# High parts of the experts' weight tiles: a rounding copy on ScalarE in place of GpSimd

## The chip, the cores and the metric

The kernel runs on one core of a Trainium2 chip. The metric is the device time of one execution in microseconds, the median of several runs; less is better. The engines are named as in the profile: PE (TensorE), DVE (VectorE), ACT (ScalarE), POOL (GpSimd), SP (SyncE, which issues the loads of the weights).

## The reference

One sequence of 512 tokens of 1024 features goes through two layers of a first block (stick breaking and sliding window attention, an MLP) and one layer of a second (a state space mixer and a sparse attention side by side, then a mixture of experts) and a last norm. All is float32. What the change concerns is the mixture of experts:

```python
p_group = softmax(tf @ w_rg + b_rg);  pg, gsel = top_k(p_group, 1)
pe = softmax(logits of the chosen group);  pv, pi = top_k(pe, EXPERT_TOPK)
wts = pg * pv / sum(pv)
combine = sum(one_hot(ids, N_EXPERTS) * wts[..., None], axis=1)
for e in range(N_EXPERTS):                       # 32 experts
    he = silu(t @ w_g[e]) * (t @ w_u[e])         # 1024 -> 256
    out = out + combine[:, e:e + 1] * (he @ w_d[e])
```

Each token goes to two experts of one group of eight. The kernel computes an expert only for the tokens that chose it.

## The kernel before

**Products in parts.** To keep nearly float32's precision, most products are made of fp32r operands: a value x is cut into hi (x rounded to fp32r) and lo = x - hi, and x w is taken as x hi + x lo, and so on. `split` (with `hi_pool` at line 187 on POOL or `hi_act` at line 190 on ACT for hi, and `lo_dve` at line 193 on DVE for lo) does this everywhere. With `act=False`, the default, hi is a tensor_scalar of POOL (x times 1 times 1); with `act=True` it is a copy of ACT.

**Weights.** All weights come through `Weights`, as 532 tiles of 128x1024 in one fixed order. `load` issues a tile's DMA on SP's queue; `prefetch` cuts a tile that has been loaded; `tile` hands out the next one and sees to it that the one after it is cut too. In the experts' part a tile's raw slot and its slots for parts come from `slots` and `parts`: the raw slots are a ring of 17 (tiles named S and w_st in the trace) and a few outside it, the parts go by turns into two rings, w_hi/w_lo (two slots) and m_hi/m_lo (three). `hold` keeps the experts' tiles uncut, though loaded, until the routing is under way.

**Experts.** An expert has six tiles: four with gate and up columns, two with rows of the down product. The first five are cut, the last is used whole (as fp32). So the 32 experts have 192 tiles of 512 KB and 160 cuts. `gather` builds, for a quad of experts, the matrix S (gS) that selects the tokens in their slots, on DVE (lines 1916 and 1917), multiplies it with the normalised rows on PE (ps_tr), and ACT copies the results out of two banks into xT (line 1926). `expert` multiplies xT by the gate and up tiles (ps_gu); ACT copies the result (mcp, line 1940), PE transposes it by a product with an identity (ps_pt), ACT takes Silu (mhe), DVE multiplies by the up half (lines 1947 and 1949); the hidden values are cut into mhs (hi on POOL, lo on DVE), and PE multiplies them by the down tiles (ps_po). `pair` scales two experts' rows by the tokens' weights (line 2010), and `put` scatters them to DRAM by an indirect DMA on POOL's queue.

**Before the first quad** stands the routing: `route`, a chain of small DVE steps with a few products; the normalised rows (`moe`: ACT scales, POOL adds the shift at line 2064, ACT makes hi, DVE lo); `turn`, which turns h into rows by PE and ACT. The first five tiles are cut inside `tc.issue_after(...)`, which puts what is issued within it behind the named instruction: in the kernel before, behind `chosen` (the last step of the first gS, on DVE) and `shifted` (the last addition of the shift, on POOL).

**Order.** The program gives the instructions an order of priority; a scheduler with a timeline of its own then fixes the order of each engine's queue, and each queue runs in that order, waiting by semaphores. The branch for experts with more than 64 tokens (`further`) is not entered with these inputs.

Of the kernel before, what the change touches and what calls it, by code (L numbers as in the profile page):

```python
# [11 lines left out]
F32R = mybir.dt.float32r  # L12
# [3 lines left out]
OP = mybir.AluOpType  # L16
# [12 lines left out]
# ---------------------------------------------------------------- constants  # L29
# [4 lines left out]
# 1 / theta ** (i / 64) and theta ** (-i / 64), i = 0, 2, .. 62, as float32 gives them  # L34
# [32 lines left out]
class Weights:  # L67
    """Tiles of 1024 columns per partition, taken in one fixed order."""
# [3 lines left out]
    def __init__(self, k, src, total):  # L72
        self.k, self.src, self.total = k, src, total
        self.specs = []
        self.raw, self.ready = {}, {}
        self.loaded = self.made = 0
        self.hold = total       # no tile from here on is cut yet
        self.slots = None       # a part of the program may place tile i itself: slots(i) -> raw, parts (None: not cut)
# [10 lines left out]
    def prefetch(self, upto):  # L89
        k = self.k  # L90
        self.load(upto)
        for i in range(self.made, min(upto, self.hold)):
# [10 lines left out]
            k.split(hi, lo, st)  # L103
# [29 lines left out]
class K:  # L133
# [7 lines left out]
    def phase(self, name, alias={}, nbufs={}):  # L141
        """Opens the working pools of a part of the program."""
        self.alias, self.nbufs = alias, nbufs
        ctx = ExitStack()
        self.wk = ctx.enter_context(self.tc.tile_pool(name="wk_" + name, bufs=1, reuse_waits="tile"))
        self.ps = ctx.enter_context(self.tc.tile_pool(name="ps_" + name, bufs=1, space=PSUM, reuse_waits="tile"))
        return ctx

# [5 lines left out]
    def t(self, shape, tag, dt=F32, bufs=1):  # L154
        """Kept: the slots S0.. and the constants; the rest goes when its phase ends."""
# [11 lines left out]
    def pace(self, every, back=2):  # L167
        """Beats for the products of dense units: each waits for the one `back` before it (0: none).
        They keep the queue of TensorE short, for the steps of a chain between them."""
# [19 lines left out]
    def hi_act(self, hi, x):  # L189
        self.nc.scalar.copy(hi, x)  # L190
# [18 lines left out]
    def rsqrt(self, out, v):  # L209
        """out = v ** -0.5, v [128, n]."""  # L210
        self.nc.gpsimd.tensor_tensor(out, v, self.mhalf.to_broadcast(list(v.shape)), op=OP.pow)

    def rsqrt_act(self, out, v, w, y):
        """The same by ScalarE and VectorE; w and y are scratch of the same shape (y may be out)."""
# [22 lines left out]
    def fm(self, rhs, pieces, evac):  # L237
        """A unit: 128 output features by 512 tokens."""
# [6 lines left out]
    def dense_tm(self, xh, xl, outs, pieces_of, ncols, bank_mates=1):  # L245
        """outs[tb] [128 tokens, ncols] += x[:, tb].T @ w; `bank_mates` outputs share a bank."""
# [38 lines left out]
    def norm_chunk(self, c, x, g, hi, lo):  # L285
        """x [128, 512] of chunk c: g x in two parts, and its squares into the running sum."""
# [16 lines left out]
    def norm_factor(self):  # L303
        """r[token], token major."""
# [12 lines left out]
    def norm_finish(self):  # L317
        """r[token] token major and along the free axis on all partitions."""
# [12 lines left out]
    def o_halves(self, dst, ps_lo, ps_hi, shape):  # L331
        """dst = ps_lo + ps_hi for the two 64-partition halves of a bank."""
# [5 lines left out]
# ---------------------------------------------------------------- first block  # L338
class Block1:
    # dense units between the steps of the stick breaking attention  # L340
    PRE = 6
    PLAN = {3: ("q", 4), 4: ("q", 5), 6: ("g", 6), 7: ("q", 6), 8: ("q", 7), 10: ("g", 7)}
    PACE = (3, 2)       # of the dense units, but for the first
# [88 lines left out]
    def swa_turn(self, tb):  # L432
        """Transposes of q and k of one token block."""
# [75 lines left out]
    def swa(self, r):  # L509
        """Token blocks in a pipeline of four stages, dense units between them."""  # L510
# [154 lines left out]
    def attend(self, xh, xl):  # L665
        """xh, xl [128, 8*512]: parts of g x; the running sum of squares is in k.ssq."""
# [23 lines left out]
    def merge(self, xs, gt, rb):  # L690
# [16 lines left out]
        for m in range(8):  # L707
            g1 = g1s[m // 2][:, m % 2]

            def both(m=m, g1=g1):  # L710
                a, b = k.bank("w2", 2, (P, 2, 512)), None
                # the two branches fill one tile of eight blocks
# [21 lines left out]
    def out_and_mlp(self, ms, x_src, next_norm, between=()):  # L734
        """x_src: DRAM [128, 8, 512]; next_norm(c, x_c) takes each finished chunk of the new x;
        `between` is work for the gaps between the units."""
# [54 lines left out]
G, HG = 4, 8          # state space groups, heads in each  # L791
# [3 lines left out]
def shape_constants2():  # L795
    i = np.arange(P)
    causal = np.where(i[:, None] > i[None, :], np.float32(NEG), np.float32(0))   # [s, t]
# [19 lines left out]
def vec_layout(inp):  # L817
    """Small vectors, features on partitions."""
# [12 lines left out]
class Block2:  # L831
# [7 lines left out]
    def row(self, name, at, n, tag):  # L839
        """A vector of the input on all partitions."""  # L840
# [33 lines left out]
    def scale(self, c, x):  # L874
        """x of chunk c by the first norm's gain."""
# [3 lines left out]
    def norm(self, x, rb, hi, lo):  # L879
        """Parts of the first modulated norm, chunk by chunk, of x by the gain."""  # L880
        k, nc = self.k, self.k.nc
        for c in range(KC):
# [3 lines left out]
            if c == KC - 1:  # L886
                # its gain comes here, and not in place: it is still on its way to DRAM
# [8 lines left out]
    def begin(self, hh, hl):  # L896
        """Steps of the state space and gates of the attention, for all tokens."""
# [20 lines left out]
    def ssm_steps(self):  # L918
        """The step sizes, and the decays' running sums within a chunk, tokens on partitions."""
# [26 lines left out]
    def ssm_begin(self):  # L946
        k, nc = self.k, self.k.nc
        # the running sums along the free axis
# [10 lines left out]
        # dt x by parts, beside zeros, so that two heads fill the partitions of a product  # L959
# [11 lines left out]
    def ssm_units(self, g, room):  # L971
        """Units of a group's projections: B, C, four of x, four of z; room(i) takes the i-th."""
# [16 lines left out]
    # units taken ahead of the attention's end, whose results wait in DRAM  # L989
    AHEAD = {0: range(10), 3: range(8, 10)}  # L990
    PACE = (4, 2)       # of the dense units between the attention's steps
# [34 lines left out]
    def ssm_scan(self, g, xz, bc):  # L1026
# [3 lines left out]
        BC = s6[:, 0:2048].rearrange("p (a b t) -> p a b t", a=2, b=2)      # B, C by parts  # L1030
# [5 lines left out]
        def front(ck):  # L1036
            """What no state enters: dt x by parts, D x, and the decayed products of C and B."""
# [30 lines left out]
        for ck in range(4):  # L1068
# [33 lines left out]
            for b in range(2):  # L1102
                # two pairs of heads: features on partitions, the products with both parts of M side by side
# [25 lines left out]
    def ssm_norm(self, g, xz, ssq):  # L1129
        """Norm over the group's features, by parts."""  # L1130
# [45 lines left out]
    def ssm(self):  # L1176
        """The state space, and the gated sum of both mixers by parts."""
# [26 lines left out]
    def gate_units(self, col, tag):  # L1204
        """Columns of the input projection before their sigmoid: the tile, and the units that fill it."""
# [14 lines left out]
    def rotations(self, work):  # L1220
        """cos | cos and -sin | sin of every token and frequency."""
# [29 lines left out]
    def rotate(self, dst, src, tb, n, tmp):  # L1251
        """dst [128, n, 64] = src turned by position."""
# [8 lines left out]
    def by_token(self, hh, hl, cols, n, tag="d"):  # L1261
        """x @ columns of the input weights, tokens on partitions, n <= 256 columns."""
# [7 lines left out]
    def nsa_keys(self, sw, kr, tb):  # L1270
        """Keys of both groups, by parts, each twice over the partitions."""
# [12 lines left out]
    def nsa_values(self, br, src, tb):  # L1284
        """Values of the selected branch by parts, those of the window whole."""
# [37 lines left out]
    def blocks(self, kcT, vcT):  # L1323
        """Blocks of keys and values with their position vectors, by parts: [128, key or value, 16, 2, 64]."""
# [19 lines left out]
    def compress(self, blocks, more):  # L1344
        k, nc = self.k, self.k.nc
        # both parts of the blocks on the partitions, then their sum turned
# [23 lines left out]
        hv = k.t([P, 2, 2, 2, P], "hidv", F32R)         # each value block's columns four times  # L1370
# [23 lines left out]
        # values of the compressed blocks, once for each of four heads, beside zeros  # L1394
# [889 lines left out]
```

## Time and profile before

| | |
|---|---|
| median of 3 runs | 2909.4 us (2905.84 to 2910.61) |
| profiled execution: span from first to last instruction | 2902.1 us |
| mean granted TensorE clock over the span | 0.978 |
| PE busy | 2737.3 us (94%) |
| DVE busy | 1893.7 us (65%) |
| POOL busy | 1330.9 us (46%) |
| ACT busy | 840.2 us (29%) |
| moved over the span | 355.47 MB, 122 GB/s |

The page gives busy time over the whole span, in which stages with different limits follow one another: the first block, the two mixers, and from about 2440 us the routing and the experts. A view by stretches shows a stage by itself. The view of waits says who stood, for how long, and what ended it. A timeline row is a start, a duration, the engine, the line, the operation with output and inputs, the shape, and how many like it follow one another; in brackets stands the engine's idle time ahead of it and what ended that. The granted clock is a share of 2.4 GHz: 1.00 is the upper level and a half the lower, and values between are means over a stretch with both.

### The profile page before, as it was taken

The page shows a single profiled execution, that of the slowest core. Times are in us where ns is not written, and L with a number is a line of the kernel's source. Part 1 is how long each engine was busy: PE and PEld are TensorE (multiplying, and loading weights), DVE is VectorE, ACT ScalarE, POOL GpSimd, SP SyncE. Part 2 cuts the span into 40 slices and gives each one's busy share as a digit, 9 for nine tenths or more (in the row PEclk, how much of TensorE's full clock was granted, in tenths as well). Part 3 has the DMA queues.
Part 4 walks back from the last instruction along what each step waited for, and adds up shares of the span by engine and source line. Part 5 has one row for each costly group of instructions (what it writes and reads, how often), then busy time and mean ns, then how long its engine had stood idle before and what let it go on. Part 6 is the DMA issues. An engine that isn't in the chain of part 4 may idle for free. (4 is left out here: it accounts for less than half of the span.)

```text
span 2902.1 us, 36642 instructions
## 1 busy us (share of the span) xinstructions
PE 2737.3 (94%) x13452; PEld 2211.3 (76%) x13452; DVE 1893.7 (65%) x2911; ACT 840.2 (29%) x1684; POOL 1330.9 (46%) x1718
## 2 busy tenths in 40 slices
PE   7999999999999999999989999999999997888886
PEld 6788788888878877778869887768787876666664
DVE  6865553334486656556545785668677765999898
ACT  3444221021144441201112354462442333211111
POOL 4544244142355423423323454446655652565665
PEclk9999999999999999999999999999999998999988
DMA  4111332223211124556442411222121252677765
GB/s 136 56 61 51 116 95 95 95 99 112 101 59 59 50 96 147 172 176 196 154 154 95 134 56 48 91 85 77 66 80 66 76 211 77 223 270 262 257 236 207
DMA packets 108875, 355.47 MB, mean 122 GB/s; under 512 B 19495, under 2 KB 20391, under 8 KB 108048
## 3 DMA queue, kind: packets, MB, share of 16 engines
q1 hardware_dynamic: 105056, 342.71, 35.3%
q0 software_dynamic: 2592, 6.15, 0.6%
q10 hardware_dynamic: 1040, 4.19, 0.4%
q8 instruction: 108, 1.77, 0.3%
q14 instruction: 79, 0.65, 0.1%
HBM read 329.51 MB, written 27.26 MB: 123 GB/s over the span
## 5 line engine op out<-in xcount | busy, mean ns | idle before, releaser
L165 PE MATMUL ps_d<-S,w_hi 128*128 128x512 f32 x4448 | 1421.0, 397 | 18.6 <-POOL c_eps L181 5.7
L165 PEld LDWEIGHTS ps_d<-S,w_hi 128*128 128x128 f32 x4448 | 827.7, 188 | 204.4 <-POOL c_eps L181 12.2
L165 PE MATMUL ps_d<-S,w_lo 128*128 128x512 f32 x2224 | 877.0, 396 | 14.9 <-DVE w_lo L193 14.6
L187 POOL TENSOR_SCALAR w_hi<-w_st 128x1024 fp32r<-128x1024 f32 x343 | 389.3, 1135 | 743.3 <-PE ps_d L165 610.6
L193 DVE TENSOR_TENSOR w_lo<-w_st,w_hi 128x1024 fp32r<-128x1024 f32 x343 | 453.8, 1323 | 295.4 <-POOL w_hi L187 273.3
L165 PEld LDWEIGHTS ps_d<-S,w_lo 128*128 128x128 f32 x2224 | 418.8, 188 | 112.9 <-DVE w_lo L193 23.2
L203 ACT ACTIVATE f<-ps_d 128x512 f32<-128x512 f32 x64 | 38.4, 600 | 457.3 <-PE ps_d L165 457.3
L181 POOL MEMSET c_eps<- 1x1 f32 x424 | 35.7, 89 | 233.9 <-PE ps_d L165 197.0
L187 POOL TENSOR_SCALAR m_hi<-S 128x1024 fp32r<-128x1024 f32 x81 | 118.4, 1466 | 52.8 <-PE ps_po L165 22.7
L187 POOL TENSOR_SCALAR S<-of 128x512 fp32r<-128x512 f32 x96 | 105.7, 1101 | 67.5 <-DVE of L728 31.3
L193 DVE TENSOR_TENSOR m_lo<-S,m_hi 128x1024 fp32r<-128x1024 f32 x81 | 124.4, 1549 | 13.8 <-POOL m_hi L187 13.8
L862 DVE SCALAR_TENSOR_TENSOR W<-wada,W 128x1024 f32<-128x1024 f32 x48 | 68.5, 1426 | 97.8 <-DMA wada<-in_w_ada_t 97.8
L1501 POOL TENSOR_SCALAR pw<-pw,ri,gn 128x128 f32<-128x128 f32 (+3 forms) x128 | 90.5, 714 | 54.9 <-DVE ri L1500 49.9
L165 PE MATMUL ps_tr<-gS,S 128*128 128x256 f32 x512 | 87.3, 311 | 24.0 <-DVE gS L1917 24.0
L165 PEld LDWEIGHTS ps_tr<-gS,S 128*128 128x128 f32 x512 | 77.9, 208 | 35.8 <-issue 30.4
L193 DVE TENSOR_TENSOR S<-of,S 128x512 fp32r<-128x512 f32 x96 | 79.5, 828 | 33.0 <-POOL S L187 31.0
L165 PE MATMUL ps_w<-w_hi,S 128*128 128x512 f32 x256 | 83.6, 406 | 10.5 <-POOL w_hi L187 10.5
L193 DVE TENSOR_TENSOR w_lo<-S,w_hi 128x1024 fp32r<-128x1024 f32 x53 | 85.9, 1626 | 2.2 <-POOL w_hi L187 2.2
L187 POOL TENSOR_SCALAR w_hi<-S 128x1024 fp32r<-128x1024 f32 x53 | 68.6, 1296 | 26.8 <-PE ps_gu L165 26.8
L165 PE MATMUL ps_w<-S,w_hi 128*128 128x512 f32 x256 | 80.7, 395 | 0.0
L203 ACT ACTIVATE pw<-pw,mx 128x128 f32<-128x128 f32 (+3 forms) x128 | 71.4, 559 | 29.7 <-DVE mx L1498 28.9
L165 PE MATMUL ps_po<-m_hi,mhs 128*128 128x512 f32 x128 | 50.4, 435 | 29.9 <-DVE mhs L193 24.3
(565 smaller groups left out, 4850.2 us busy)
## 6 DMA issues: line engine op xcount, KB each, us to landing
w_st<-in_w SPq DMA_DIRECT2D x374, 512.0 KB, 3.3
S<-in_w SPq DMA_DIRECT2D x158, 512.0 KB, 4.9
wada<-in_w_ada_t SPq DMA_DIRECT2D x48, 512.0 KB, 3.6
x<-S SPq DMA_DIRECT2D x16, 256.0 KB, 2.0
moe_rows<-S ACTq DMA_DIRECT2D x1, 4096.0 KB, 16.5
ssm_away<-nf SPq DMA_DIRECT2D x12, 256.0 KB, 2.0
S<-in_x_t SPq DMA_DIRECT2D x8, 256.0 KB, 6.9
S<-in_x_t SPq DMA_DIRECT2D x1, 2048.0 KB, 8.0
```

The source lines that it names most:

```text
L165: return self.nc.tensor.matmul(out, l, r, start=start, stop=stop, skip_group_check=sk)
L181: b = self.nc.gpsimd.memset(self.beat_at[:, i:i + 1], 0.0)
L187: self.nc.gpsimd.tensor_scalar(hi, x, 1.0, 1.0, op0=OP.mult, op1=OP.mult)
L193: return self.nc.vector.tensor_tensor(lo, x, hi.bitcast(F32), op=OP.subtract)
L203: i = self.nc.scalar.activation(out, x, f, bias=bias, scale=scale, **kw)
L862: nc.vector.scalar_tensor_tensor(junk, w, 1.0, self.cs, op0=OP.mult, op1=OP.mult, accum_out=self.ada[:, j:j + 1])
L1501: nc.gpsimd.tensor_scalar(w, w, ri[:, c], gate[:, c], op0=OP.mult, op1=OP.mult)
```

## The change

hi of the experts' weight tiles is made by ACT: `Weights` gets a flag `act`, false until `moe` sets it, which `prefetch` hands to `split`. The first five cuts are put behind `turned`, the last hi that ACT made by then (that of the last block of the normalised rows), where it was `shifted`; `chosen` stays. The hi of mhs and all cuts ahead of the experts stay where they are. The rest of the diff takes comments out.

```diff
 class Weights:
     def __init__(self, k, src, total):
...
-        self.hold = total       # no tile from here on is cut yet
-        self.slots = None       # a part of the program may place tile i itself: slots(i) -> raw, parts (None: not cut)
+        self.hold = total
+        self.slots = None
+        self.act = False
...
     def prefetch(self, upto):
...
-            k.split(hi, lo, st)
+            k.split(hi, lo, st, act=self.act)
             self.ready[i] = (hi, lo)
...
     def hi_act(self, hi, x):
-        self.nc.scalar.copy(hi, x)
+        self.last_hi = self.nc.scalar.copy(hi, x)
...
     def moe(self, h, hm, out):
...
-            shifted = nc.gpsimd.tensor_tensor(f, f, shift, op=OP.add)
+            nc.gpsimd.tensor_tensor(f, f, shift, op=OP.add)
             k.split(self.hn_tm[0][:, tb], self.hn_tm[1][:, tb], f, act=True)
...
         self.turn(h, put)
+        turned = k.last_hi
...
         tile0 = len(k.W.specs)
+        k.W.act = True
...
                 k.W.hold = k.W.total
-                with k.tc.issue_after(self.chosen.ins), k.tc.issue_after(shifted.ins):
+                with k.tc.issue_after(self.chosen.ins), k.tc.issue_after(turned.ins):
                     k.W.prefetch(tile0 + 5)
```

## Rows read from the trace of the kernel before

**Rows 1.** Busy time by stretch: start:end, length, busy us (instructions), clock, DMA share, GB/s.
```profile
core 0: us, PE busy (x) PEld busy (x) DVE busy (x) ACT busy (x) POOL busy (x), PEclk, DMA share, GB/s
2472.00:2872.00 400.00, 343.15 (x1617) 263.82 (x1618) 360.36 (x357) 72.96 (x196) 249.10 (x202) 0.93 0.74 250
...
2670.00:2680.00 10.00, 7.96 (x33) 7.21 (x34) 8.11 (x11) 1.02 (x3) 2.13 (x3) 0.66 0.60 205
```
**Rows 2.** Waits of PE, 2472 to 2872: who, for whom, total us, times, longest.
```profile
PE ps_tr L165 <- DVE gS L1917: 24.0, 6, 6.3
PE ps_po L165 <- DVE mhs L193: 22.0, 9, 3.3
PE ps_gu L165 <- DVE m_lo L193: 6.5, 12, 0.7
PE ps_po L165 <- POOL mhs L187: 5.6, 4, 2.1
```
**Rows 3.** Groups on DVE, 2472 to 2872: shapes, count, busy us, mean ns, idle before.
```profile
L193 DVE TENSOR_TENSOR m_lo<-S,m_hi 128x1024 fp32r<-128x1024 f32 x81 | 124.4, 1549 | 13.8 <-POOL m_hi L187 13.8
L193 DVE TENSOR_TENSOR w_lo<-S,w_hi 128x1024 fp32r<-128x1024 f32 x53 | 85.9, 1626 | 2.2 <-POOL w_hi L187 2.2
L193 DVE TENSOR_TENSOR mhs<-mhe,mhs 128x64 fp32r<-128x64 f32 x31 | 44.7, 1442 | 14.1 <-POOL mhs L187 13.8
L1917 DVE SCALAR_TENSOR_TENSOR gS<-moe_c,gq,gS 128x256 fp32r<-128x256 f32 x31 | 27.0, 914 | 0.0
...
L1949 DVE TENSOR_TENSOR mhd<-mhe,ps_pt 128x64 f32<-128x64 f32 x31 | 6.5, 209 | 0.0
```
**Rows 4.** Timeline, 2640 to 2692: rows of DVE, then of POOL.
```profile
2645.64 3.06 DVE L193 TENSOR_TENSOR mhs<-mhe,mhs 128x64 fp32r<-128x64 f32 x1 [1.23 <-POOL mhs L187]
...
2655.58 2.05 DVE L193 TENSOR_TENSOR w_lo<-S,w_hi 128x1024 fp32r<-128x1024 f32 x1
...
2647.59 1.03 POOL L187 TENSOR_SCALAR m_hi<-S 128x1024 fp32r<-128x1024 f32 x1
...
2655.50 1.05 POOL L187 TENSOR_SCALAR m_hi<-S 128x1024 fp32r<-128x1024 f32 x1
2656.51 2.02 POOL L187 TENSOR_SCALAR w_hi<-S 128x1024 fp32r<-128x1024 f32 x1
```
**Rows 5.** Timeline ahead of the first gather: rows of ACT, then of DVE.
```profile
2464.29 2.03 ACT L190 CAST S<-S 128x1024 fp32r<-128x1024 f32 x2
...
2463.79 1.22 DVE L193 TENSOR_TENSOR S<-S,S 128x1024 fp32r<-128x1024 f32 x1
...
2471.45 1.67 DVE L1917 SCALAR_TENSOR_TENSOR gS<-moe_c,gq,gS 128x256 fp32r<-128x256 f32 x4
```
**Rows 6.** Groups on ACT, 2472 to 2872, as in Rows 3.
```profile
L1926 ACT CAST S<-ps_tr 128x256 fp32r<-128x256 f32 x128 | 43.2, 377 | 117.4 <-PE ps_tr L165 100.2 <-PE ps_gu L165 16.6
L1940 ACT COPY mcp<-ps_gu 128x512 f32<-128x512 f32 x32 | 18.8, 588 | 105.1 <-PE ps_gu L165 105.1
...
L203 ACT ACT_TABLE_LOAD x1 | 1.3, 1283 | 0.0
```
**Rows 7.** Timeline of the routing: a row of POOL, then of DVE.
```profile
2459.24 2.21 POOL L187 TENSOR_SCALAR m_hi<-S 128x1024 fp32r<-128x1024 f32 x2
...
2458.29 1.25 DVE L1845 TENSOR_TENSOR st<-A,moe_c 128x256 f32<-128x256 f32 x1
...
2462.82 0.40 DVE L1845 TENSOR_TENSOR st<-A,C 128x256 f32<-128x256 f32 x1
```
**Rows 8.** Waits of SP's queue, 2520 to 2850; then a stretch as in Rows 1.
```profile
SPq L85 <- DVE w_lo L193: 115.9, 48, 9.1
...
2380.00:2390.00 10.00, 8.29 (x29) 6.23 (x28) 4.26 (x4) 0.85 (x2) 2.71 (x2) 0.83 1.00 390
```
**Rows 9.** Groups on POOL, 2472 to 2872, as in Rows 3.
```profile
L187 POOL TENSOR_SCALAR m_hi<-S 128x1024 fp32r<-128x1024 f32 x78 | 115.1, 1479 | 52.8 <-PE ps_po L165 22.7 <-DMA S<-in_w 19.3 <-PE ps_gu L165 6.4
L187 POOL TENSOR_SCALAR w_hi<-S 128x1024 fp32r<-128x1024 f32 x51 | 66.4, 1306 | 26.8 <-PE ps_gu L165 26.8
```

## What the change will do to the time

> **What bounds the kernel now.** The change touches one stage: the 32 experts, where 192 weight tiles of 128x1024 are loaded and 160 of them are cut into a high part (hi: rounded to fp32r) and a low part (lo: what is left). So I read the profile from that stage, not from the page's averages, on which PE is the fullest engine.
>
> First the busy time by stretch, from the first gather of tokens (2472 us) to the last expert's products (2872 us) [rows 1]. In these 400 us PE is busy 343.15, DVE 360.36, POOL 249.10, ACT 72.96, and the 16 DMA engines 74%. DVE is the fullest and PE has 56.9 us of idle time; the granted clock is 0.93 in the mean, and 0.66 in the 10 us that follow a long stop of PE. So PE loses in two ways: it stands, and afterwards it runs slowly. Its work at full clock is about 343 x 0.93 = 319 us: an estimate of the floor that PE sets for this stretch.
>
> Then who ended PE's idle time [rows 2]: the selection matrix gS of the next gather (24.0 us), the low part of an expert's hidden values mhs (22.0), lo parts of weights (6.5) and the high part of mhs (5.6). These four are 58 us, all that PE stands (the first of the waits begins a little ahead of 2472). Every one is an output of DVE or POOL; none of ACT.
>
> Then why DVE is late [rows 3]. A lo part of 128x1024 takes 1549 ns in the mean in one ring and 1626 in the other. The lo of mhs, of 64 columns only, takes 1442 ns, while the product beside it with as many columns takes 209. The time is no arithmetic. The timelines show what it is [rows 4]: a lo takes 2.05 us at 2655.58 where POOL makes hi parts at the same time (1.05, then 2.02), and the lo of mhs takes 3.06 from 2645.64 and ends as the last of a run of POOL's hi parts ends (2647.59 + 1.03). DVE and POOL stop each other. Ahead of the stage [rows 5], while POOL does nothing, a lo takes 1.22 us although ACT runs a cast of the same size at the same time (two in 2.03), and gS's second step takes 1.67/4 = 0.42 against 0.914 in [rows 3].
>
> The Trainium skill ("SBUF — State Buffer", "Who interferes with whom") says that a VectorE instruction with two SBUF inputs contends with a GpSimd instruction that reads SBUF, that the loser blocks until the other has finished, and that ACT waits for nobody. The mutual stop agrees with [rows 4], but the loser's price does not: by the rule the lo of mhs would wait for one hi at most (an estimate of some 1.0 + 0.2 us) and the row shows a wait for a run of them, 3.06. By the rule alone the gain on mhs would be at most 31 x 1.0; the sum below goes by the rows.
>
> **What the change does, part by part.**
>
> (a) 160 hi parts leave POOL. On DVE, 160 lo at 1.22 instead of some 1.57 gives back 160 x 0.35 = 56 us; 31 lo of mhs at about 0.21 (their neighbour of the same size, [rows 3]) instead of 1.44, 38 us; 31 steps of gS at 0.42 instead of 0.91, 15 us. DVE falls from 360 to some 250 us. What stays on POOL (the 64-column hi of mhs, the scattering of rows) still stops DVE now and then; I leave 5 us for it. DVE is then far below PE's 319 and bounds nothing.
>
> (b) PE gets its idle time back, bounded above by all of it: 400 - 319 = 81 us (56.9 of idle, 24 of clock). Below, the bound is nothing, if something else comes late in DVE's place.
>
> (c) ACT gets 160 casts. At 2.03/2 = 1.02 us each [rows 5] that is 163 us: 73 + 163 = 236 us of load, under PE's floor, so ACT bounds by its sum nothing either. But its queue runs in order, and ACT also brings PE what it needs [rows 6]: 128 copies out of the gather's banks (377 ns) and 32 of mcp, which the transposing products wait for (588). Silu (one per expert) stands between them, and its table is loaded once in the whole stage (x1): casts and copies between Silus force no further load. A copy that comes ready behind a running cast waits up to 1.02 us, on average half of that, and it meets a cast in 163/340 of the cases: 0.24 us. With 32 mcp, 32 Silus and 64 pairs of gather copies this is 128 x 0.24 = 31 us if PE has nothing else meanwhile, and 0 if the next expert's products or the next gather fill each gap. No row shows a cast among these copies; I take half, 16 us, since gathers and products do stand mixed on PE, and keep 0 to 31 for the range.
>
> (d) The chain of a weight tile (hi, lo, product) gets no longer: 1.02 on ACT instead of 1.05 to 2.0 on POOL, then 1.22 on DVE instead of up to 2.05. The five slots for parts stay.
>
> (e) The start. The first five hi parts stand on POOL at 2456 to 2461.4, in the middle of the routing, and stretch its small DVE steps [rows 7]: one that takes 0.40 us after POOL has finished takes 1.25 beside it. Some four such steps on the chain to the first gather, at 0.8 each: 3 us. Now they wait behind the last cast of the normalised rows on ACT ("turned" names that cast, not the turning), and on DVE still behind the last step of gS. ACT has room for 5 x 1.02 before the gather's first copy, because it waits there; I cost them at nothing, and at 5 us if they stood in front of that copy.
>
> The loads on SP's queue are not edited. Their issues wait for lo parts to free the raw slots, 115.9 us for one ring alone, and in a 10 us stretch the DMA engines have carried 390 GB/s [rows 8]. The experts' 192 x 0.524 MB = 100.7 MB need 258 us at that rate; at the stage's own 250 GB/s with 74% busy, 296 us. Both are under PE's floor, so a faster lo only lets SP issue earlier.
>
> Sum for the stage: 319 (work) + 16 (copies behind casts) + 9 (rest: the first gather, the last experts, POOL's remainder, a clock not always full) = 344, against 400: 56 us. With (e): 59. The profiled execution has a span of 2902.1; the median of the runs is 2909.4, 7.3 more, which I take as unchanged: 2909.4 - 59 = 2850.
>
> **Rivals.**
>
> *Slower: ACT stands at the head of its queue.* POOL waits in front of hi parts, with 52.8 us idle ahead of one group and 26.8 ahead of another [rows 9], mostly for PE to free a slot. If ACT stands there instead with mcp, Silu and gather copies queued behind a cast that cannot begin, PE waits for ACT, and ACT for PE's slot. Price: all of these 79.6 us and the 31 of (c) on PE's path: 319 + 111 = 430, 30 over the 400, less 3: 2936. It decides from the point where more than 81 of the 111 us reach PE. Against it: both what frees a slot and what fills mcp or a gather's bank are products of the one queue of PE, so a cast that waits for a slot mostly has things behind it that come later anyway. For it: these 79.6 us are there, and POOL had little queued behind that anyone needed, while ACT has much. A chance of 0.06.
>
> *Half-way: the delays behind casts are not covered,* and part of the slot waits reaches PE: 31 + some 20 to 40 us on top of 319, so 370 to 390: 2876 to 2896. 0.16.
>
> *The port is not the reason, or the change does not relieve it:* lo stays at 1.57 beside whatever runs, DVE stays at 360, and only (e) is left: 2906. Against it [rows 5]. 0.04.
>
> *Everything is covered:* PE runs at its floor, 81 + 3: 2825. 0.06.
>
> *The DMA becomes the bound:* by busy share 296 us, so it would have to lose another 50 us to show; it lies inside the forecast's own range.
>
> **How the numbers follow.** The forecast, PE-bound with (c) between 0 and 31 and the rest between 4 and 20, is 323 to 370 for the stage and has 0.68: 2829 to 2876. The time is that of its middle, 2850. To the range come all covered and most of half-way: 2825 to 2892. Faster by over 0.2% (6 us, about what a measurement of this kernel tells from no change): 0.68 + 0.16 + 0.06 = 0.90; within: 0.04; slower: 0.06.
>
> **What would show it.** After the change, lo parts should take 1.2 us throughout, the lo of mhs a quarter of a microsecond, and hardly a row of the timeline should have 2.05. DVE should be near 250 us of a stage of about 344, ACT near 236, PE over 90% with a granted clock near 1. The waits of PE for gS and mhs should be nearly gone, and new ones, for ACT's copies (gather banks, mcp) should appear, some 10 to 30 us. If PE waits over 80 us for ACT, the first rival is right; if lo parts still take 1.5, the port was the wrong reason; if the DMA share passes 0.95 with POOL, ACT and DVE all waiting for loads, the loads are the bound.

## The result and the profile after

The changed kernel takes 2829.57 us (median of four runs, 2827.9 to 2831.93), the kernel before beside it 2908.05: a ratio of 0.9732, with an interval of 0.972 to 0.9743. That is 78.5 us faster. The forecast of 2850 had the direction, and the time lies inside its range of 2825 to 2892, but near its lower end: a gain of 59 us was forecast.

The two profiled executions differ by about as much, 2902.1 and 2826.0 us of span. Cut at three points that both kernels have, the 76.1 us are found in one place:

| stretch | before | after | difference |
|---|---|---|---|
| start to the token factors (`r_v`), ahead of all that is changed | 2438.4 | 2434.6 | -3.9 |
| factors to the first gather | 33.6 | 31.9 | -1.7 |
| first gather to the end of the span | 430.0 | 359.5 | -70.5 |
| of it, as far as the last transposing products (`ps_pt<-mcp`), "the stage" below | 400.7 | 326.8 | -73.9 |
| of it, the rest | 29.4 | 32.7 | +3.3 |

The first line is scatter and no effect: the two programs have the same order of instructions there, and in the profiles of the kernels below that share this order the stretch ended anywhere from 2434.2 to 2445.2. The +3.3 of the last line is mostly where the cut falls: eight products of the last expert but one (the two runs of four `ps_po` products from 2794.29 to about 2797.2) stand behind the cut after and ahead of it before.

The page's line of busy times, after:

```profile
span 2826.0 us, 36570 instructions
PE 2711.1 (96%) x13452; PEld 2195.5 (78%) x13452; DVE 1781.5 (63%) x2911; ACT 991.6 (35%) x1844; POOL 1129.6 (40%) x1558
```

The busy time of the stage (columns as in [rows 1]):

```profile
2466.48:2793.30 326.82, 315.11 (x1615) 248.32 (x1616) 250.86 (x357) 219.79 (x352) 51.61 (x47) 1.00 0.87 306
```

Beside [rows 1]: DVE falls from 360 to 250.9 us, POOL from 249 to 51.6, ACT rises from 73 to 219.8. PE is now the fullest, 315 of 326.8 us, at a mean granted clock of 1.00, the upper of its two levels (2.4 GHz; 0.93 in the first 20 us, 1.00 behind them), where it had been 0.93 over the stage. All the waits of PE in that stretch, as in [rows 2]:

```profile
PE ps_po L166 <- POOL mhs L188: 7.8, 11, 1.2
PE ps_tr L166 <- DVE gS L1918: 4.0, 1, 4.0
PE ps_gu L166 <- ACT m_hi L191: 1.1, 3, 0.4
PE ps_tr L166 <- DVE S L194: 1.1, 1, 1.1
PE ps_pt L166 <- ACT mcp L1941: 0.9, 1, 0.9
PE ps_gu L166 <- ACT w_hi L191: 0.7, 1, 0.7
PE ps_po L166 <- DVE mhs L194: 0.5, 1, 0.5
```

The 24.0 us for gS are one wait of 4.0 (the first gather's, which begins ahead of the stage), the 22.0 for the lo of mhs are 0.5, the 6.5 for lo parts of weights are gone. ACT, which now makes the hi of every weight tile, holds PE up for 2.7 us in all (1.1, 0.9 and 0.7).

Groups of DVE, ACT and POOL from 2466 to 2796 (columns as in [rows 3]; the lines have moved by one):

```profile
L194 DVE TENSOR_TENSOR m_lo<-S,m_hi 128x1024 fp32r<-128x1024 f32 x81 | 98.9, 1222 | 35.2 <-ACT m_hi L191 29.9 <-PE ps_po L166 4.3 <-issue 0.7
L194 DVE TENSOR_TENSOR w_lo<-S,w_hi 128x1024 fp32r<-128x1024 f32 x53 | 64.6, 1221 | 15.2 <-ACT w_hi L191 11.6 <-DMA S<-in_w 2.1 <-DMA w_st<-in_w 1.4
...
L1918 DVE SCALAR_TENSOR_TENSOR gS<-moe_c,gq,gS 128x256 fp32r<-128x256 f32 x32 | 13.8, 478 | 0.0
...
L194 DVE TENSOR_TENSOR mhs<-mhe,mhs 128x64 fp32r<-128x64 f32 x31 | 9.1, 295 | 5.2 <-POOL mhs L188 3.5
...
L191 ACT CAST m_hi<-S 128x1024 fp32r<-128x1024 f32 x78 | 82.2, 1054 | 38.4 <-PE ps_gu L166 20.2 <-PE ps_po L166 15.8 <-DMA S<-in_w 1.0
L191 ACT CAST w_hi<-S 128x1024 fp32r<-128x1024 f32 x51 | 53.8, 1057 | 11.0 <-PE ps_gu L166 5.9 <-DMA S<-in_w 2.2 <-DVE mhd L1950 1.7
...
L1941 ACT COPY mcp<-ps_gu 128x512 f32<-128x512 f32 x32 | 18.6, 583 | 1.5 <-PE ps_gu L166 1.5
...
L188 POOL TENSOR_SCALAR mhs<-mhe 128x64 fp32r<-128x64 f32 x31 | 27.4, 883 | 137.5 <-DVE mhe L1948 96.9 <-DVE mhd L1950 40.5
```

A lo part has gone from 1549 and 1626 ns to 1222 and 1221, the lo of mhs from 1442 to 295, a step of gS from 914 to 478 [rows 3]. One row has got worse, the hi of mhs, which stays on POOL: 883 ns in the mean, where it had been 407 (the row of before, from 2472 to 2872):

```profile
L187 POOL TENSOR_SCALAR mhs<-mhe 128x64 fp32r<-128x64 f32 x31 | 12.6, 407 | 30.1 <-DVE mhe L1947 28.5 <-DMA S<-in_w 1.3
```

The timeline of after shows how:

```profile
2593.54 1.21 DVE L194 TENSOR_TENSOR w_lo<-S,w_hi 128x1024 fp32r<-128x1024 f32 x1
2593.58 2.41 POOL L188 TENSOR_SCALAR mhs<-mhe 128x64 fp32r<-128x64 f32 x1 [5.56 <-DVE mhe L1948]
2594.67 1.21 DVE L194 TENSOR_TENSOR m_lo<-S,m_hi 128x1024 fp32r<-128x1024 f32 x1
...
2596.46 0.24 POOL L188 TENSOR_SCALAR mhs<-mhe 128x64 fp32r<-128x64 f32 x1 [0.47 <-DVE mhe L1948]
```

The same operation takes 2.41 us beside two lo in a row and 0.24 by itself. The stop of [rows 4] is still there, with the roles exchanged and 31 small operations instead of 160 large ones to meet it.

SP's queue still waits for lo parts to free raw slots (2500 to 2780), at a DMA share of 0.87:

```profile
SPq L86 <- DVE m_lo L194: 87.2, 66, 3.4
SPq L86 <- DVE w_lo L194: 57.5, 27, 3.4
```

### The profile page after: what moved, and what is told of

It is laid out like the page before. It is cut to its first block, busy times and chain, and to the rows that moved or that the text cites. A ratio compares the mean times of both kernels' runs of the same rounds, so it can differ in the third digit from the quotient of the medians.

```text
span 2826.0 us, 36570 instructions
## 1 busy us (share of the span) xinstructions
PE 2711.1 (96%) x13452; PEld 2195.5 (78%) x13452; DVE 1781.5 (63%) x2911; ACT 991.6 (35%) x1844; POOL 1129.6 (40%) x1558
## 4 chain that ended last, share of the span: by engine, by line
PE 76%; DVE 8%; POOL 5%; DMA 5%; issue 4%; ACT 2%; SPq 0%; DVEq 0%; POOLq 0%; ACTq 0%
PE ps_d L166 45%; PE ps_w L166 8%; PE ps_o L166 5%; PE ps_b L166 4%; DMA wada<-in_w_ada_t 3%; PE ps_gu L166 3%; PE ps_po L166 3%; DVE w_lo L194 2%; PE ps_e L166 2%; PE ps_tr L166 2%; PE ps_tr L1511 1%; PE ps_s L166 1%; POOL w_hi L188 1%; POOL mhs L188 1%; POOL S L1149 1%
## 5 line engine op out<-in xcount | busy, mean ns | idle before, releaser
L188 POOL TENSOR_SCALAR w_hi<-w_st 128x1024 fp32r<-128x1024 f32 x332 | 371.6, 1119 | 740.3 <-PE ps_d L166 612.9
L194 DVE TENSOR_TENSOR w_lo<-w_st,w_hi 128x1024 fp32r<-128x1024 f32 x343 | 447.5, 1305 | 300.7 <-POOL w_hi L188 275.0
L194 DVE TENSOR_TENSOR m_lo<-S,m_hi 128x1024 fp32r<-128x1024 f32 x81 | 98.9, 1222 | 35.2 <-ACT m_hi L191 29.9
L191 ACT CAST m_hi<-S 128x1024 fp32r<-128x1024 f32 x81 | 85.2, 1053 | 38.4 <-PE ps_gu L166 20.2
L166 PE MATMUL ps_tr<-gS,S 128*128 128x256 f32 x512 | 80.7, 297 | 4.1 <-DVE gS L1918 4.0
L166 PEld LDWEIGHTS ps_tr<-gS,S 128*128 128x128 f32 x512 | 71.7, 193 | 16.3 <-issue 6.7
L188 POOL TENSOR_SCALAR mhs<-mhe 128x64 fp32r<-128x64 f32 x31 | 27.4, 883 | 137.5 <-DVE mhe L1948 96.9
L2017 POOL DMA_INDIRECT moe_rows<-my,idx x14 | 19.1, 1363 | 142.9 <-DVE my L2011 135.1
L194 DVE TENSOR_TENSOR w_lo<-S,w_hi 128x1024 fp32r<-128x1024 f32 x53 | 64.6, 1221 | 15.2 <-ACT w_hi L191 11.6
```

The source lines that it names most:

```text
L166: return self.nc.tensor.matmul(out, l, r, start=start, stop=stop, skip_group_check=sk)
L188: self.nc.gpsimd.tensor_scalar(hi, x, 1.0, 1.0, op0=OP.mult, op1=OP.mult)
L191: self.last_hi = self.nc.scalar.copy(hi, x)
L194: return self.nc.vector.tensor_tensor(lo, x, hi.bitcast(F32), op=OP.subtract)
L2017: self.k.nc.gpsimd.indirect_dma_start(out=self.Y, out_offset=bass.IndirectOffsetOnAxis(ap=self.idx[:, j:j + 1], axis=0), in_=y, in_offset= ...
```

## The experiments

Each kernel is timed beside the kernel before on the same chip; the ratio is to that. "To the end" is the time from the first gather to the end of the span, which has no cut in it. The busy times are of the stage.

| kernel | median us | ratio, interval | to the end | stage | PE | DVE | ACT | POOL | clock |
|---|---|---|---|---|---|---|---|---|---|
| after | 2829.57 | 0.9732, 0.972 to 0.9743 | 359.5 | 326.8 | 315 | 251 | 220 | 52 | 1.00 |
| after again | 2830.2 | 0.9728, 0.9703 to 0.9752 | 357.0 | 325.6 | 315 | 251 | 220 | 52 | 1.00 |
| e1 gate only | 2901.66 | 0.9993, 0.9983 to 1.0002 | 430.8 | 401.4 | 346 | 360 | 73 | 246 | 0.92 |
| e2 ACT only | 2820.79 | 0.9706, 0.969 to 0.9722 | 351.7 | 322.2 | 312 | 255 | 221 | 35 | 0.98 |
| e2 again | 2823.56 | 0.9701, 0.9679 to 0.9723 | 352.1 | 322.4 | 312 | 255 | 221 | 35 | 0.98 |
| e3 POOL reads | 2925.19 | 1.007, 1.0053 to 1.0086 | 439.4 | 406.8 | 350 | 333 | 221 | 259 | 0.90 |
| e4 POOL writes | 2838.09 | 0.9773, 0.9757 to 0.979 | 365.6 | 332.3 | 320 | 258 | 220 | 200 | 0.98 |
| e5 two rings | 2837.07 | 0.9748, 0.9721 to 0.9776 | 360.7 | 330.7 | 319 | 292 | 164 | 125 | 0.98 |
| e6 more on ACT | 2830.26 | 0.9732, 0.971 to 0.9753 | 356.7 | 323.7 | 318 | 254 | 296 | 42 | 0.98 |
| e7 mhs on ACT | 2833.22 | 0.9744, 0.9722 to 0.9766 | 361.4 | 333.2 | 319 | 259 | 224 | 34 | 0.97 |
| e8 shift on DVE | 2828.37 | 0.9719, 0.9699 to 0.974 | 356.9 | 326.0 | 315 | 252 | 219 | 51 | 0.99 |
| e12 shift on DVE, early | 2829.46 | 0.9727, 0.9708 to 0.9747 | 356.5 | 325.6 | 316 | 251 | 219 | 53 | 0.99 |
| e10 all on ACT | 2836.35 | 0.9747, 0.9725 to 0.9768 | 356.7 | 325.4 | 315 | 251 | 220 | 51 | 1.00 |

### Which half of the change: e1 and e2

The change has two halves: the engine of the hi parts, and the point from which the first five may begin. e1 keeps the late start and leaves hi on POOL:

```diff
-        k.W.act = True
+        k.W.act = False
```

> The kernel before (hi parts on POOL) with the new place alone: the first five are put behind ACT's last cast of the normalised rows, by the order of issue. Theory: an order of issue binds within an engine's queue alone as far as the rows show (POOL's first hi began at 2456 while the step of DVE that it was put behind ended at 2473), so POOL begins them at about the same time as before or a few us later: 2900 to 2910, at best the 3 us of part (e). Rival: the new place is what matters for the start, and gives 4 to 6 us by itself: 2902 to 2904, with the routing's steps at 0.2 to 0.4 us.

The stage is that of before (401.4 us, DVE 360, POOL 246), and so is the time within 0.2%. The new starting point by itself is worth nothing that can be measured. It did not hold POOL back either: the five hi ran ahead of the shift's additions there (the last of them ended at 2440.4, the additions began at 2442.62), so an order of issue that names an instruction of ACT did not bind POOL here.

e2 has hi on ACT and the old starting point, POOL's last addition of the shift:

```diff
-            nc.gpsimd.tensor_tensor(f, f, shift, op=OP.add)
+            shifted = nc.gpsimd.tensor_tensor(f, f, shift, op=OP.add)
...
-                with k.tc.issue_after(self.chosen.ins), k.tc.issue_after(turned.ins):
+                with k.tc.issue_after(self.chosen.ins), k.tc.issue_after(shifted.ins):
```

> The changed kernel with the first five cuts put behind POOL's last addition of the shift, as in the kernel before, and all hi parts on ACT. Theory: the engine is what matters; ACT has idle time before the first gather's copies, 2828 to 2833. Rival: without the new place the casts get in between ACT's copies of the rows and its casts of the normalised rows, and the first gather begins up to 5 us later: 2832 to 2836.

So the whole gain is the engine's. e2 is the fastest version run, faster than either range of its expectation. It and the changed kernel were measured once more, on other chips:

> The kernel of e2_act_only once more, beside the two others: ratio 0.969 to 0.972, some 2815 to 2823, if its 6 us below the changed kernel are no accident of one chip.

> The changed kernel as it is, once more, beside the runs of the kernel before on this chip, so that the others of this set have a neighbour: ratio 0.972 to 0.975, some 2826 to 2834.

The ratios of e2 are 0.0026 and 0.0027 below those of after, some 8 us, in both pairs, though the intervals overlap; e2 is likely the better of the two. In the traces 5.3 us (31.9 against 26.6) lie between the factors and the first gather, and 5 to 8 behind it. The first part can be read. The routing in after: a row of POOL, then of DVE:

```profile
2442.98 9.27 POOL L2065 TENSOR_TENSOR S<-S,g 128x1024 f32<-128x1024 f32 x4 [5.52 <-ACT g L1760]
...
2443.26 2.14 DVE L1803 TENSOR_TENSOR eq<-le,m 128x32 f32<-128x32 f32 x1
2445.43 2.26 DVE L1779 TENSOR_TENSOR fo_s<-eq,moe_c 128x32 f32<-128x32 f32 x1
```

and in e2, where three hi stand on ACT ahead of the copies of g for which the additions wait:

```profile
2449.21 2.92 ACT L191 CAST m_hi<-S 128x1024 fp32r<-128x1024 f32 x3
...
2453.27 10.66 POOL L2065 TENSOR_TENSOR S<-S,g 128x1024 f32<-128x1024 f32 x4 [8.36 <-ACT g L1760]
```

In after the shift's additions begin 8.4 us behind the factors and meet the routing: two steps of 32 columns take 2.14 and 2.26 us. They did the same in the kernel before, also 8.4 us behind the factors, and the two steps took as long there:

```profile
2446.85 9.25 POOL L2064 TENSOR_TENSOR S<-S,g 128x1024 f32<-128x1024 f32 x4 [5.53 <-ACT g L1759]
...
2447.12 2.13 DVE L1802 TENSOR_TENSOR eq<-le,m 128x32 f32<-128x32 f32 x1
2449.29 2.26 DVE L1778 TENSOR_TENSOR fo_s<-eq,moe_c 128x32 f32<-128x32 f32 x1
```

In e2 the additions begin 11.3 us behind the factors; these two steps are over by then (2448.99 and 2449.22) and take 0.19 us each.

### Is it the meeting of POOL and DVE: e3 and e4

e3 lets POOL read every raw tile once more, as before, into a scratch that nobody reads, while ACT makes the hi parts that count:

```diff
             k.split(hi, lo, st, act=self.act)
+            if self.act:
+                junk = k.t([P, 1024], "c_rope", mybir.dt.bfloat16)
+                k.hi_pool(junk, st)
```

> The changed kernel, and beside each hi part that ACT makes POOL reads the same raw tile once more and writes a copy (128x1024, as bf16) that nobody uses. Theory (port): the gain came from DVE and POOL no longer stopping each other when both read SBUF. Then the added reads bring lo parts back to 1.45 to 1.6 us in the mean, DVE to 340 us or more in the experts' stage, and the time to 2885 to 2915. Rival (lateness): hi parts were late because POOL made them late, in a queue with other work, and lo parts and products only followed. Then an operation that nobody waits for costs nothing: 2828 to 2836, lo parts at 1.22.

Groups from 2466 to 2866:

```profile
L197 DVE TENSOR_TENSOR m_lo<-S,m_hi 128x1024 fp32r<-128x1024 f32 x77 | 112.2, 1461 | 23.1 <-ACT m_hi L194 22.9
...
L197 DVE TENSOR_TENSOR mhs<-mhe,mhs 128x64 fp32r<-128x64 f32 x30 | 24.8, 825 | 23.8 <-POOL mhs L191 22.8
...
L191 POOL TENSOR_SCALAR c_rope<-S 128x1024 bf16<-128x1024 f32 x123 | 172.8, 1405 | 73.9 <-DMA S<-in_w 66.8
```

Lo is back at 1461 ns and the whole gain is gone, though ACT does all that it does in after. It went past the mark: 1.007, 20 us slower than before. Two waits of PE in the stage (2482 to 2889):

```profile
PE ps_po L169 <- POOL mhs L191: 25.1, 11, 4.1
PE ps_tr L169 <- DVE gS L1921: 20.1, 13, 9.4
```

With the smaller ones (11.4, 3.5, 3.0 and 1.5) PE waits 39.5 us for DVE, where it waited 5.6 in after. The 25.1 are a second cost: POOL now also stands 66.8 us at the head of its queue for loads, as the third row says, and the hi of mhs comes behind these reads. A third lies ahead of the stage: factors to first gather take 40.9 us, 9.0 more than in after. So e3 shows that POOL's reading makes DVE slow again and lets PE wait for it; how much of the lost time that is by itself, its time does not show.

e4 keeps POOL as busy, with operations that only write:

```diff
             k.split(hi, lo, st, act=self.act)
+            if self.act:
+                for _ in range(2):
+                    junk = k.t([P, 512], "c_rope")
+                    k.nc.gpsimd.memset(junk, 0.0)
```

> The changed kernel, and beside each hi part POOL only writes: two memsets of 128x512 float32 into a tile that nobody uses, about 1.1 us together and so as long as a hi part took. If what stops DVE is POOL's reading, lo parts stay at 1.22 us and the time at 2828 to 2838. If any work of POOL on SBUF stops DVE, lo parts rise to 1.4 or more and the time to 2870 to 2910, as with the reads.

Groups from 2466 to 2866:

```profile
L108 POOL MEMSET c_rope<- 128x512 f32 x300 | 159.1, 530 | 15.7
...
L198 DVE TENSOR_TENSOR m_lo<-S,m_hi 128x1024 fp32r<-128x1024 f32 x81 | 100.9, 1247 | 30.4 <-ACT m_hi L195 27.8 <-PE ps_gu L170 1.3 <-PE ps_tr L170 1.2
L198 DVE TENSOR_TENSOR w_lo<-S,w_hi 128x1024 fp32r<-128x1024 f32 x53 | 64.4, 1219 | 8.3 <-ACT w_hi L195 8.1
...
L1921 DVE TENSOR_SCALAR gS<-moe_c,gq 128x256 fp32r<-128x256 f32 x32 | 15.3, 536 | 0.0
```

POOL has 200 us of work in the stage, and lo stays at 1247 and 1219 ns. A busy POOL does not stop a lo; a reading POOL does. The Trainium skill ("SBUF — State Buffer", "Who interferes with whom") says just this of a VectorE instruction with two SBUF inputs: it meets a GpSimd instruction that reads, not one that only writes. Here the traces agree, 1461 against 1219 to 1247. PE waits 7.1 us for DVE in that stage, not 39.5 as in e3. The time, 2838.09, is at the upper end of what was expected for this case. The first step of gS, which has one tensor as its input, goes from 354 ns in after to 536 (it was 491 before). e4's stage is 5.5 us longer than that of after: 4.8 are PE's own busy time (319.9 against 315.1) at a granted clock of 0.98, 0.8 its idle time. The longest waits of PE there are for the hi of mhs, which now stands behind memsets:

```profile
PE ps_po L170 <- POOL mhs L192: 10.4, 5, 4.3
```

In after they were 7.8 in all and 1.2 at the longest.

### Does time on DVE turn into time of the kernel: e5

If a microsecond of DVE were a microsecond of the kernel, three of five hi parts on ACT would give about three fifths of the gain. If PE's floor decides, they give nearly all of it, as soon as DVE is below it. e5 puts the `m_hi` ring on ACT and leaves the `w_hi` ring on POOL:

```diff
-        self.act = False
+        self.act, self.cuts = False, -1
...
-            k.split(hi, lo, st, act=self.act)
+            if self.act:
+                self.cuts += 1
+            k.split(hi, lo, st, act=self.act and self.cuts % 5 in (1, 3, 4))
```

> The changed kernel with two of five hi parts (those of the ring w_hi) back on POOL and three on ACT. Theory (port): the price goes with the number of POOL's reads: 64 of the 160 reads, 40% of the 75 us, so 2855 to 2875, lo parts at 1.3 to 1.4 us in the mean. Rival (a threshold: DVE has room to spare up to PE's floor, and DVE and POOL collide only as long as DVE is the bound): DVE at some 300 us stays under PE's 319, so PE hides it: 2828 to 2842.

Groups from 2470 to 2800:

```profile
L196 DVE TENSOR_TENSOR m_lo<-S,m_hi 128x1024 fp32r<-128x1024 f32 x81 | 110.6, 1370 | 12.3 <-ACT m_hi L193 11.5 <-PE ps_gu L168 0.5
L196 DVE TENSOR_TENSOR w_lo<-S,w_hi 128x1024 fp32r<-128x1024 f32 x53 | 72.1, 1362 | 4.7 <-POOL w_hi L190 4.7
```

Lo stands between the two states, DVE has 292 us instead of 251, and the stage is 330.7: 3.9 us longer for 41 us more on DVE. The linear price (2855 to 2875) is refuted; the time, 2837.07, is in the range of the rival, in which PE's floor decides.

### Does a full ACT cost: e6, e7 and e10

The forecast charged 16 us for copies that stand behind casts. e6 adds a copy of 128x512 to every tile on ACT, whose result nobody reads:

```diff
             k.split(hi, lo, st, act=self.act)
+            if self.act:
+                junk = k.t([P, 512], "c_rope")
+                k.nc.scalar.copy(junk, st[:, 0:512])
```

> The changed kernel with a further copy on ACT for each hi part, 128x512 of the raw tile into a tile that nobody uses, some 0.53 us behind the cast: 160 x 0.53 = 85 us more on ACT, 306 of a stage of 330. Theory 1: ACT's queue costs PE nothing until its sum passes PE's floor, since the order is made for it: 2828 to 2840. Theory 2 (part (c) of the prediction: each copy for PE stands behind a cast for half its length): the chance to meet ACT busy rises from a half to over nine tenths, 128 x (0.45 + ...) us on PE in full: 2850 to 2890.

```profile
2475.93:2799.62 323.69, 317.89 (x1623) 251.70 (x1624) 253.75 (x358) 295.65 (x512) 41.80 (x48) 0.98 0.87 309
```

Its one wait of PE for ACT in that stretch:

```profile
PE ps_pt L169 <- ACT mcp L1944: 0.2, 1, 0.2
```

ACT is 295.65 of 323.69 us busy, 91%, and PE waits 0.2 us for it. The time is that of after, and the second theory of the expectation (2850 to 2890) fails. What stands behind casts on ACT does so without a price that shows.

e7 takes the last work of the split from POOL, the hi of mhs:

```diff
-        k.split(hp[:, 0, own], hp[:, 1, own], he[:, 0], act=last)
+        k.split(hp[:, 0, own], hp[:, 1, own], he[:, 0], act=True)
```

> The changed kernel with the hi of mhs on ACT too (31 more casts of 128x64, 0.25 us each). What is left of PE's waits is led by this hi on POOL, 7.8 us in 11 waits, where POOL takes 883 ns in the mean for it because DVE's lo parts now hold it up. If these waits are on the path, 5 to 8 us less than the changed kernel: 2822 to 2825. If ACT then brings it as late, or PE's next wait takes over: 2828 to 2832.

No gain: PE's 7.8 us for POOL's mhs become 2.5 for ACT's, but now hi parts of weights come late, 4.8 us in one ring (below) and 1.3 in the other:

```profile
PE ps_gu L166 <- ACT m_hi L191: 4.8, 4, 1.3
...
PE ps_po L166 <- ACT mhs L191: 2.5, 1, 2.5
```

ACT is less loaded here than in e6 (224 of 333 us), and yet PE waits 8.6 us for it. The likely reason, which no run isolates, is what stands at the head of its queue: a small operation that waits for a product of the Silu, with hi parts behind it.

e10 makes all hi parts of the kernel on ACT, also in the dense stages:

```diff
-        self.act = False
+        self.act = True
```

> The changed kernel with the hi parts of all weight tiles on ACT, also ahead of the experts (372 more, some 1.05 us each: 390 us of POOL's work). There PE is busy 97 to 100% of most stretches already, so a faster lo gives little: theory, 2815 to 2832, by the few waits for lo and hi that are left (some 15 us). Rival: in the attention and the state space ACT's exponentials stand on the chain, and casts ahead of them cost more than the lo parts give: 2835 to 2880.

```profile
400.00:800.00 400.00, 399.09 (x1803) 327.89 (x1802) 158.35 (x194) 127.69 (x177) 55.54 (x69) 1.00 0.30 99
```

In this dense stretch PE is 399.09 of 400 us busy (398.35 in after): there is nothing to give back in it, and the kernel is if anything slower than after (0.0015 to 0.0019 of the ratio, 4 to 6 us, with intervals that overlap). The theory's 2815 to 2832 is missed; 2836.35 lies at the low end of the rival's range. In the profiled run, the longest of its four (2844.69), the loss is ahead of the experts: the factors come at 2453.7 us, later than in any other profile here, and what follows takes as long as in after (31.9 and 356.7). Whether it is ACT's casts on the chain of the mixers, as the rival has it, no run isolates.

### The start: e8 and e12

If the additions of the shift stop the routing's steps, they can go to DVE:

```diff
-            nc.gpsimd.tensor_tensor(f, f, shift, op=OP.add)
+            nc.vector.tensor_tensor(f, f, shift, op=OP.add)
```

> The changed kernel with the four additions of the shift (128x1024, two inputs in SBUF) on DVE instead of POOL. In the changed kernel POOL takes 9.27 us for them at 2443, and four routing steps of DVE beside them take 2.1 to 2.3 us each instead of 0.2. Theory (port, in the routing): the steps fall to 0.2, DVE takes four additions of 1.2 us more, partly off the chain: from r_v to the first gather 31.9 us becomes 25 to 28, the time 4 to 7 us less than the changed kernel, 2820 to 2826. Rival: the four additions stand in DVE's queue ahead of the chain and give it all back: 2828 to 2832.

```profile
2453.69 2.35 DVE L2065 TENSOR_TENSOR S<-S,g 128x1024 f32<-128x1024 f32 x2
2456.06 2.35 DVE L2065 TENSOR_TENSOR S<-S,g 128x1024 f32<-128x1024 f32 x2
```

Four additions take 4.7 us instead of POOL's 9.27, behind the routing's first steps, and factors to first gather falls from 31.9 to 27.7. The total does not show these 4 us clearly: the ratio is 0.0009 to 0.0013 below that of after, some 3 to 4 us, and the intervals are wider than that. The time lies in the range of the rival, but not for its reason, since the start did get shorter. e12 also lets the casts begin early:

```diff
-                with k.tc.issue_after(self.chosen.ins), k.tc.issue_after(turned.ins):
+                with k.tc.issue_after(self.chosen.ins):
```

> As e8_shift_dve, and the first five cuts put only behind the last step of the first gS, not behind ACT's casts of the rows: ACT may make them ahead of the routing, as in e2_act_only. If the start of e2_act_only (26.6 us from r_v to the first gather) came from POOL's additions moving out of the routing's way, this is the same as e8_shift_dve within 3 us: 2820 to 2826. If the early casts have a worth of their own, 2814 to 2820.

27.6, the same, and a time within 1.1 us: early casts have no worth of their own that shows, and what e2 wins at the start (26.6) comes, but for some 1 us, from the additions moving out of the routing's way.

## Why the prediction was right, and where its size was off

**What bounds.** Right. The stage was bound by DVE, and DVE by meeting POOL's reads: PE's waits for DVE, 57.0 us before and 5.6 after, are 39.5 with the reads put back (e3) and 7.1 with writes in their place (e4); each sum has the first gather's wait of 4.0 to 9.4 us in it. One reading of it was loose: the four waits that the prediction calls all that PE stands are 58.1 us, of which some 6.2 lie ahead of 2472, and four smaller ones, 4.9 us, complete the 56.9.

**(a)** Right. DVE at "some 250" is 250.9, lo at 1.22 is 1.222, gS at 0.42 is 0.478, the lo of mhs at 0.21 is 0.295; the last two miss by 32 x 0.058 + 31 x 0.085 = 4.5 us, about the 5 that were left for POOL's remainder. The first step of gS, which was not in the sum, gave 32 x 0.137 = 4.4 us back (491 to 354 ns), so that the 250 came out as exactly as it did by luck.

**(b)** Right, with a floor a little high: PE has 315.1 us of work at a clock of 1.00, not 319. That e5 gets nearly all of the gain with DVE at 292 speaks for the floor, and not DVE's busy time, as what sets the price.

**(c)** This is the term that was mis-sized: 16 us taken, between 0 and 31. PE waits 2.7 us for ACT in after and 0.2 in e6, where ACT has 76 us more to do. The step that failed is "I take half": the bound 0 had its reason in the same part (the next expert's products and the next gather fill the gaps), and it was the value to take, since half had no row. By the ledger: 344 forecast, 326.8 measured, 17.2 less, of which 13.3 are (c) (16 less 2.7) and 3.9 the floor. The remaining 9 us came out as 9.0, PE's other idle time (326.8 - 315.1 - 2.7), but that is luck: 7.8 us of waits are for POOL's hi of mhs, which DVE's lo parts now hold up, and the forecast had POOL stopping DVE there and not the reverse.

**(d)** Right: no new wait of PE for lo parts.

**(e)** Right in kind: 3 us were forecast and 1.7 measured. Of the steps that the five hi stretched, two stand before the products that the first gather needs: den, which is in front of As in DVE's queue, and As itself. Before and after:

```profile
2456.07 1.07 DVE L1866 TENSOR_SCALAR den<-m 128x4 f32<-128x4 f32 x1
...
2457.36 1.01 DVE L1821 TENSOR_TENSOR As<-A 128x128 f32<-128x128 f32 x1
```

```profile
2452.22 0.16 DVE L1867 TENSOR_SCALAR den<-m 128x4 f32<-128x4 f32 x1
...
2452.66 0.29 DVE L1822 TENSOR_TENSOR As<-A 128x128 f32<-128x128 f32 x1
```

As ends 19.9 us behind the factors before and 18.4 after, and these 1.6 us (19.94 less 18.39) are nearly all of the 1.7. The two others that got short (1.25 and 0.99 before, 0.42 and 0.15 after) come behind As and hardly count. What the forecast did not look at is the larger stop in the same place, the shift's additions on POOL, which stretch four steps to 2.1 to 2.3 us in both kernels alike: counted from the factors, the first gather comes 5.3 us sooner than in after with the additions 2.9 us later (e2), and 4.2 with them on DVE (e8).

**The rivals.** What came was in effect "everything is covered", 2825 with a chance of 0.06, which was too little beside a forecast whose main difference from it was an unmeasured half. The half-way rival fell with (c). The slower rival saw a true row and drew the wrong end from it: ACT does stand at the head of its queue for PE's slots (20.2 + 15.8 + 5.9 us in the groups above), and PE hardly waits for it (2.7 us). The reason that the prediction put against this rival fits; no run tests it. e7 may be where a trace of that mechanism shows, 8.6 us. "The port is not the reason" is excluded by e3 and e4. The loads do not bound: 0.87 of the DMA engines' time at 306 GB/s, where e2 reaches 0.89 and 317, and SP still waits for lo parts.

**The loser's price.** Against the rule that the loser blocks for the whole of the other's instruction (the Trainium skill, "SBUF — State Buffer", "Who interferes with whom") the prediction held that a loser waits for a run. The changed kernel shows it from the other side: POOL's 64 columns, begun at 2593.58 behind one lo, end at 2595.99, past a second lo that began at 2594.67. Read as a wait for one instruction, the rule would have let them end some 0.24 behind the first lo (2594.75), at about 2595.0.

**What stays open.** Behind the first gather e2 is 5 to 8 us shorter than after (351.7 and 352.1 against 359.5 and 357.0). Its hi of mhs take 369 ns instead of 883 (the row of e2 again):

```profile
L188 POOL TENSOR_SCALAR mhs<-mhe 128x64 fp32r<-128x64 f32 x31 | 11.4, 369 | 161.1 <-DVE mhe L1948 120.2 <-DVE mhd L1950 38.2 <-DMA my<-moe_rows 2.4
```

and PE waits 1.4 us for them instead of 7.8. That would be the size, but e6 has them at 407 ns and 356.7 us to the end, no shorter than after again. Whether the small operations fall beside lo parts probably depends on the phase in which the stage starts; no run isolates that, and the cause of e2's 5 to 8 us stays open.

## What to carry to other kernels

Where two engines are both busy, read whether their same-size operations take longer side by side than alone, before the arithmetic is blamed: here 1.22 against 1.55 to 1.63 us, and a 64-column step of 0.3 against 1.4, cost some 70 us in a stage of 400. Move the work to the engine that meets nobody, and price what is left by the next floor, not by the microseconds taken from the old bound: a DVE that was 41 us fuller, but still below PE, cost 4. And ask of an in-order queue what stands at its head, not only how full it is: ACT's, 91% busy, held PE up for 0.2 us in e6, and at 67% for 8.6 in e7, where a small operation was put into it.

## What the hardware showed that was not expected

- POOL's writes leave a two-input DVE operation alone (1219 to 1247 ns with 159 us of memsets beside it), its reads do not (1461); a one-input step of 128x256 was slowed by the memsets, 354 to 536 ns.
- The loser changes with the traffic. Beside a run of POOL's hi parts DVE lost (3.06 us for 64 columns); beside two of DVE's lo parts in a row POOL lost (2.41 us for 64 columns).
- ACT's cast of 128x1024 takes 1054 ns in the mean whatever DVE and POOL do beside it: 1054 in e3 and 1051 in e5, with POOL reading.
- The same instructions ahead of the change took between 2434.2 and 2445.2 us in different profiles, so an effect of a few microseconds is to be read from a stretch, not from the span.
